# Layer A's three Strassen products: weight sums made of additions only, half of them by accumulating DMAs for 14 of 24 weight pairs

## The chip, the cores and the metric

One core of a Trainium2 chip runs the whole program. The metric is the device time in microseconds, as the median over runs. Engines are named as the profile names them: PE multiplies matrices, DVE is the vector engine, ACT the scalar engine, POOL is GpSimd (here it mostly issues DMAs), SP issues most of the loads.

## The reference

A trunk of two layers over 512 positions of width 2048, in float32. Only layer A matters here:

```python
proj = x @ w_in
q, k, v, gate, iq, ik, iw = jnp.split(proj, SPLITS_A, axis=-1)
...
o = from_blocks(lax.map(block_fn, (to_blocks(q), to_blocks(iq), to_blocks(iw), starts)))
return (o * jax.nn.silu(gate)) @ w_o
```

Three blocks of 512 output columns of `x @ w_in` are the subject: the second and third block of the gate, and the fourth block of the queries.

## The kernel before, in words

Every matrix product is made of float32 numbers split in two parts: `split` (line 142) makes the high part on ACT (a copy) and the low part on DVE (a subtraction), and `mm3` (line 146) issues three matmuls for each product of two split numbers. All instructions issued inside these helpers carry line 118 in the profile; the matmuls carry lines 147 to 149.

The order of PE's work is the program's. ACT and DVE keep program order for what is issued while `pinned` is set, and that holds for all that is told here. The DMAs of POOL are placed by the scheduler; POOL itself issues in order.

The three products of layer A (lines 1136 to 1155) are made by a Strassen-Winograd scheme. A 2048 x 512 block of weights is cut in two halves of rows and two halves of columns, and a product of 2x2 blocks is made with seven block products in seven PSUM banks instead of eight. The sums of the activations, four for each of eight rows of 128, were made earlier and lie split in SBUF. The sums of the weights are made as the weights arrive.

`strassen_items` (line 444) makes them. A unit is one pair of weight rows, 128 rows k and 128 rows k + 8 by 512 columns: one 512 KB load into a `raw` buffer, of which there are three. There are 8 units in a product, 24 in all; the texts number them 0 to 23. With q0, q1 the two column halves of row k and q2, q3 those of row k + 8, `prepare` (line 449) makes two sums on DVE, and the loop makes two more from these:

```python
dve.tensor_tensor(st[:, :, 0], two[0], two[2], ALU.add)
dve.tensor_tensor(st[:, :, 2], two[1], two[0], ALU.subtract)
...
dve.tensor_tensor(s2, s1, two[1], ALU.subtract)
dve.tensor_tensor(s4, two[3], s2, ALU.subtract)
```

The sums of a unit lie in a place of 128 x 1024 numbers, one of three that other work has left free: the two halves of F[0] (`two`, line 1096) and `t3`. Then, for each half of 128 columns, q1 to q3 and the four sums are split. After the second half's splits, `prepare` of the next unit follows (except at units 1, 9 and 17). `Ahead(..., 2)` keeps two halves, one unit, ahead of PE. `gemm_s` (line 557) takes one half after the other and issues seven `mm3` for each: 42 matmuls of 256 columns for a unit, 336 for a product. Its third pair of factors is the first that needs a sum.

Side work is taken from the deque `bg` at chosen steps of a product (`PUMPS`, line 1131; a step is one `mm3`, a product has 112). At the end of a product `combine` (line 583) copies three of the seven banks by ACT and adds the rest on DVE, which frees the banks for the next product; its five last additions, four SiLU and, for the two gate blocks, a 1 MB store by POOL (`held_g`, line 1155) go to `bg`. During the second product keys are transposed on PE (line 1118). At the start of the third, POOL loads half of a query block into F[0]'s first half (line 1148), and after it the other half (line 1157); the first reader of F[0] is `first_query` (line 1313), some steps into the next stage. `turned_rows` (line 978) ends with four small DMAs by POOL.

Of the kernel before, what the change touches and what calls it, by code (L numbers as in the profile page):

```python
# [51 lines left out]
def steps(gen, n):  # L52
    for _ in range(n):
        next(gen, None)
# [23 lines left out]
def trunk_kernel(  # L78
# [115 lines left out]
    def next_raw():  # L194
        while sent[0] < len(units) and len(raws) < (6 if homes and sent[0] in kv_units else 2 if sent[0] == 3 else 4 if 5 < sent[0] < 24 else 3):
            lent = kv_units.get(sent[0], 0)
            if sent[0] in first_units:
                raw = x_places[first_units[sent[0]] % 2]
            elif homes and lent % 2:
                raw = homes[lent // 2 % 3]  # L200
            else:
                raw = top.tile([128, 2, 512], F32, name="raw", tag="raw", bufs=3)
            unit = units[sent[0]]
            if len(unit) == 1:
                _, k, n = unit[0].shape
            else:
                k, n = 2, unit[-1]
            raw = raw.rearrange("p a n -> p (a n)")[:, : k * n].rearrange("p (k n) -> p k n", k=k)
            if len(unit) == 1:
                nc.sync.dma_start(raw, unit[0])  # L210
            else:
                src, a, b, c0, n = unit
                rows = src.rearrange("(k p) n -> p k n", p=128)
                step = b - a
                if sent[0] < 2:

                    for i, cut in enumerate(((0, H if sent[0] else NSEL, T), (0, T))):
                        for lo, hi in zip(cut, cut[1:]):
                            halves.append((raw[:, i, lo:hi], rows[:, a + i * step, c0 + lo : c0 + hi]))
                    if len(halves) == 6:  # L220
                        for n in (3, 5):
                            tc.keep_in_program_order(nc.scalar.dma_start(*halves[n]))
                        for n in (1, 4, 2, 0):
                            nc.sync.dma_start(*halves[n])
                elif isinstance(c0, tuple):

                    for half, out in enumerate(raw.rearrange("p k (h n) -> h p k n", h=2)):
                        at = D // 2 * half + c0[0]
                        nc.sync.dma_start(out, rows[:, a : b + 1 : step, at : at + n // 2])
                else:  # L230
                    loaded = nc.sync.dma_start(raw, rows[:, a : b + 1 : step, c0 : c0 + n])
                    if 2 < sent[0] < 6:
                        tc.keep_in_program_order(loaded)
            raws.append(raw)
            sent[0] += 1
        return raws.popleft()
# [244 lines left out]
    def strassen_stream(widths, wp, places=None):  # L481
        return Ahead(strassen_items(widths, wp, places), 2)

    def kv_items(room, first, later, third=None):

        made = [0, 0]
        temps = list(first)

        def temp():
            made[0] += 1  # L490
            return temps[made[0] % len(temps)]

        def parts(src):
            made[1] += 1
            if room[0] and made[1] in (3, 5):
                pair = room[0].pop()
            elif (room[0] is not None and made[1] < 5) or made[1] % 2 == 0:
                pair = weight_parts()
            else:
                pair = [  # L500
                    room[1].tile([128, 4, 128], F32R, name=n, tag=n, bufs=3).rearrange("p a n -> p (a n)")
                    for n in ("sh", "sl")
                ]
            split(*pair, src)
            return pair

        for k in range(8):
            raw = next_raw()
            for a in range(2):
                yield parts(raw[:, a])  # L510
        for _ in range(2 if third is None else 0):
            st = room[1].tile([128, 4 * H], F32, name="st", tag="st", bufs=2)
            temps.extend(st[:, n * T : (n + 1) * T] for n in range(2))
        temps.extend(third or ())
        for k in range(8):
            raw = next_raw()
            s3 = temp()
            dve.tensor_tensor(s3, raw[:, 0], raw[:, 1], ALU.subtract)
            yield parts(raw[:, 0])
            yield parts(s3)  # L520

        def sums():
            r0 = next_raw()
            r1 = next_raw()
            s1, s2, s4 = temp(), temp(), temp()
            dve.tensor_tensor(s1, r0[:, 1], r1[:, 1], ALU.add)
            dve.tensor_tensor(s2, s1, r0[:, 0], ALU.subtract)
            dve.tensor_tensor(s4, r1[:, 0], s2, ALU.subtract)
            return s2, s1, s4

        temps.extend(later)
        ready = sums()
        for k in range(8):
            three = ready
            for n, src in enumerate(three):
                if n == 2 and k < 7:
                    ready = sums()
                yield parts(src)
# [38 lines left out]
    def quarter(x, i, j0=0, rows=2):  # L577

        j = j0 + rows * (i % 2 == 0)
        t = H * (i in (1, 2))  # L580
        return x[:, j : j + rows, t : t + H]

    def combine(wp, M, dst, u=None):

        m1, m2, m6, m7, m5, m3, m4 = M
        if u is None:
            u = wp.tile([128, 2, H], F32, name="u", tag="u", bufs=1)
        u = u[:, : m1.shape[1]]
        c11, c22, c12, c21 = (dst(i) for i in range(4))
        pinned[0] = True  # L590
        act.activation(u, m1, AF.Copy)
        act.activation(c21, m7, AF.Copy)
        act.activation(c22, m5, AF.Copy)
        dve.tensor_tensor(c11, m2, u, ALU.add)
        dve.tensor_tensor(u, m6, u, ALU.add)
        pinned[0] = False

        def onto(c):
            dve.tensor_tensor(c, c, u, ALU.add)

        paced(dve.tensor_tensor, c12, m3, c22, ALU.add)
        return [
            lambda: dve.tensor_tensor(c22, c22, c21, ALU.add),
            lambda: dve.tensor_tensor(c21, c21, m4, ALU.subtract),
            *(lambda c=c: onto(c) for c in (c12, c21, c22)),
        ]
# [371 lines left out]
    def turned_rows(packed, back):  # L978

        sw = pq.tile([128, T], F32, name="sw", tag="sw", bufs=1)  # L980
        swapped.append(sw)

        def last():
            dve.tensor_tensor(packed, packed, sw, ALU.add)
            for h in range(4):
                nc.gpsimd.dma_start(back(h), packed[32 * h : 32 * h + 32])

        return [
            lambda: dve.stream_shuffle(sw, packed, HALF_SWAP_16),
            lambda: dve.tensor_tensor(sw, sw, Sq, ALU.mult),  # L990
            lambda: dve.tensor_tensor(packed, packed, Cq, ALU.mult),
            last,
        ]
# [101 lines left out]

    two = [flat[0][:, 4 * n : 4 * n + 4].rearrange("p a t -> p (a t)") for n in range(2)]
    pinned[0] = True
    items = strassen_stream([512] * 3, sp, [*two * 2, t3.rearrange("p a t -> p (a t)"), two[1]]).prime()
    pinned[0] = False
    steps(gemm, 2)  # L1100
    for j in range(2):
# [13 lines left out]
    def key_rows(g, rows=slice(0, 128)):  # L1115
        return Kf[rows, :, g * 128 : (g + 1) * 128]
# [19 lines left out]
    for n, g in enumerate((1, 2, 3)):  # L1136
        M = product_banks(1 - n)
        gemm = pumped_at(gemm_s(items, C3A, M), PUMPS[n])
        if n == 1:
            bg.extend(rounds[2:])  # L1140
            steps(gemm, 28)
            for k in range(4):
                turned = turn_keys(k)
                steps(gemm, 10)
                turned()
                steps(gemm, 6)
        if n == 2:
            nc.gpsimd.dma_start(F[0][:, 0:2], held_q[0][:, 0:2])
            bg.extend(turned_rows(KP, lambda g: key_rows(g, slice(0, 32))))
        run(gemm)  # L1150
        drain()
        if n < 2:
            bg.extend(combine(None, M, lambda i: quarter(F[3], i), u[:, :, 0:H]))
            bg.extend(lambda j=j: act.activation(F[3][:, j], F[3][:, j], AF.Silu) for j in range(4))
            bg.append(lambda g=g: nc.gpsimd.dma_start(held_g[g], F[3]))

    nc.gpsimd.dma_start(F[0][:, 2:4], held_q[0][:, 2:4])
    items = Ahead(rest_items(), 2).prime()
    spare_u = pq.tile([128, T], F32, name="wk", tag="wk", bufs=1).rearrange("p (j t) -> p j t", j=2)
    late = deque(combine(None, M, lambda i: quarter(F[3], i), spare_u))  # L1160
    pc_.close()
    pkv_ = ExitStack()
    pkv = pkv_.enter_context(ss(name="pkv", bufs=1, side="right"))
# [1105 lines left out]
```

## Time and profile before

| | us |
|---|---|
| three runs, median | 1814.47 |
| three runs, lowest and highest | 1814.08, 1816.0 |
| the profiled execution, its own time | 1815.21 |
| its span, first to last instruction | 1813.5 |
| PE busy | 1807.6 |
| DVE busy | 1543.4 |
| ACT busy | 1051.5 |
| POOL busy | 33.5 |

The profile is of one execution. Times in it count from the first instruction. Matmuls are pipelined: a matmul's duration is longer than the distance to the next, so the pace of PE is read from start to start. A DMA issued by POOL appears twice, as an instruction of POOL (the issue) and as a row with the time from issue to landing. In the columns of a timeline, "x2" means two like instructions in one row, and what stands in brackets is the idle time before it and what ended that.

### The profile page before, as it was taken

The numbers are of one execution on the slowest core, as the hardware profiler recorded it, in microseconds if no ns is written. First come the engines' busy times: TensorE is split into PE (matmuls) and PEld (weight loads), VectorE is DVE, ScalarE is ACT, GpSimd is POOL, SyncE is SP. The second block draws the span as 40 slices with busy tenths as digits, with TensorE's granted clock in tenths as the row PEclk, the third lists the DMA queues.
The fourth block names the chain that finished last, engine by engine and source line by source line (L and its number), as shares of the span: only waits on it lengthen the run. The fifth ranks groups of instructions, "written<-read, shape, count | busy, mean of one in ns | idle before, by whom it ended". The sixth has DMA issues, their size and how long they took to land.

```text
span 1813.5 us, 28260 instructions
## 1 busy us (share of the span) xinstructions
PE 1807.6 (100%) x10231; PEld 1594.5 (88%) x10231; DVE 1543.4 (85%) x3085; ACT 1051.5 (58%) x1953; POOL 33.5 (2%) x75
## 2 busy tenths in 40 slices
PE   9999999999999999999999999999999999999999
PEld 8888888999888899888888899998888889988898
DVE  7888999998888899975578998888877889997997
ACT  4555355466666544575356444468888854557644
POOL 0001110000000000000000000000000000000000
PEclk9999999999999999999999999999999999999999
DMA  6524575344331454333347533322122244434453
GB/s 216 157 79 140 164 230 176 105 129 147 127 94 47 108 126 143 115 103 105 124 128 243 181 104 105 106 87 88 60 69 81 70 117 124 144 117 141 124 148 122
DMA packets 123740, 226.40 MB, mean 125 GB/s; under 512 B 10512, under 2 KB 40208, under 8 KB 122064
## 3 DMA queue, kind: packets, MB, share of 16 engines
q1 hardware_dynamic: 119936, 209.25, 38.5%
q0 software_dynamic: 3376, 14.95, 2.5%
q8 instruction: 80, 1.31, 0.3%
q14 instruction: 60, 0.49, 0.1%
q10 hardware_dynamic: 288, 0.39, 0.1%
HBM read 205.42 MB, written 16.78 MB: 123 GB/s over the span
## 4 chain that ended last, share of the span: by engine, by line
PE 99%; DMA 1%; DVE 0%; ACT 0%; issue 0%; DVEq 0%; ACTq 0%
PE m L148 12%; PE m L147 12%; PE m L149 12%; PE g L147 10%; PE g L149 10%; PE g L148 10%; PE o L148 4%; PE o L149 4%; PE o L147 4%; PE q L149 2%; PE q L148 2%; PE q L147 2%; PE iq L149 1%; PE iq L148 1%; PE iq L147 1%; PE z L2062 1%
## 5 line engine op out<-in xcount | busy, mean ns | idle before, releaser
L118 ACT ACTIVATE wh<-raw 128x512 fp32r<-128x512 f32 (+3 forms) x561 | 309.3, 552 | 373.2 <-PE g L148 118.7
L118 DVE TENSOR_TENSOR wl<-raw,wh 128x512 fp32r<-128x512 f32 (+3 forms) x560 | 331.6, 593 | 108.7 <-ACT wh L118 101.5
L147 PE MATMUL g<-xh,wh 128*128 128x512 f32 (+1 forms) x816 | 317.2, 389 | 0.0
L148 PE MATMUL g<-xl,wh 128*128 128x512 f32 (+1 forms) x816 | 314.6, 385 | 0.0
L149 PE MATMUL g<-xh,wl 128*128 128x512 f32 (+1 forms) x816 | 314.5, 385 | 0.0
L149 PEld LDWEIGHTS g<-xh,wl 128*128 128x128 f32 x816 | 153.3, 188 | 31.1
L147 PEld LDWEIGHTS g<-xh,wh 128*128 128x128 f32 x816 | 153.4, 188 | 29.1 <-ACT wk L116 0.3
L148 PEld LDWEIGHTS g<-xl,wh 128*128 128x128 f32 x816 | 153.5, 188 | 28.7
L118 ACT ACTIVATE sh<-f 128x512 fp32r<-128x512 f32 x129 | 80.5, 624 | 109.4 <-DVE f L118 104.2
L147 PE MATMUL m<-xh,wh 128*128 128x256 f32 x400 | 113.3, 283 | 0.0
L149 PE MATMUL m<-xh,wl 128*128 128x256 f32 x400 | 113.2, 283 | 0.0
L148 PE MATMUL m<-xl,wh 128*128 128x256 f32 x400 | 113.2, 283 | 0.0
L147 PE MATMUL m<-c,sh 128*128 128x256 f32 x368 | 104.3, 283 | 0.0
L149 PE MATMUL m<-c,sl 128*128 128x256 f32 x368 | 104.3, 283 | 0.0
L148 PE MATMUL m<-c,sh 128*128 128x256 f32 x368 | 104.1, 283 | 0.0
L118 DVE TENSOR_TENSOR sl<-f,sh 128x512 fp32r<-128x512 f32 x129 | 88.9, 689 | 16.1 <-ACT sh L118 16.0
L149 PE MATMUL o<-xh,wl 128*128 128x512 f32 x256 | 99.7, 389 | 0.0
L147 PE MATMUL o<-xh,wh 128*128 128x512 f32 x256 | 99.6, 389 | 0.0
L148 PE MATMUL o<-xl,wh 128*128 128x512 f32 x256 | 99.6, 389 | 0.0
L147 PE MATMUL m<-xh,sh 128*128 128x256 f32 x336 | 95.2, 283 | 0.0
L149 PE MATMUL m<-xh,sl 128*128 128x256 f32 x336 | 95.1, 283 | 0.0
L148 PE MATMUL m<-xl,sh 128*128 128x256 f32 x336 | 95.1, 283 | 0.0
(456 smaller groups left out, 4786.6 us busy)
## 6 DMA issues: line engine op xcount, KB each, us to landing
raw<-w_in_a SPq DMA_DIRECT2D x95, 512.0 KB, 3.7
raw<-w_in_b SPq DMA_DIRECT2D x64, 512.0 KB, 3.8
raw<-w_ple_gate SPq DMA_DIRECT2D x44, 512.0 KB, 3.9
raw<-w_o_a SPq DMA_DIRECT2D x24, 512.0 KB, 4.7
raw<-w_o_b SPq DMA_DIRECT2D x24, 512.0 KB, 4.7
f<-w_in_a SPq DMA_DIRECT2D x16, 512.0 KB, 4.6
f<-w_kv_b SPq DMA_DIRECT2D x16, 512.0 KB, 4.8
raw<-w_kv_b SPq DMA_DIRECT2D x16, 512.0 KB, 4.5
```

Of the source, the lines that this page charges most:

```text
L118: ins = method(*args, **kw)
L147: pe.matmul(out, a[0], b[0], start=start, stop=False)
L148: pe.matmul(out, a[0], b[1], start=False, stop=False)
L149: pe.matmul(out, a[1], b[0], start=False, stop=stop)
L2062: pe.matmul(z, down if kb % 2 else tri, p, start=False, stop=n == 1, skip_group_check=True)
```

## The change

`added_items` takes the place of `strassen_items` in these three products. Its four sums are q0 + q1, q0 + q2, q0 + q2 + q1 and q0 + q2 + q1 + q3, without a subtraction; `combine_added` takes the changed signs into account, with the same number of instructions as `combine`. For units 7 to 20 the first two sums are not made on DVE. POOL issues three DMAs for such a unit, two units ahead: one writes q0 from DRAM to two neighbouring blocks of the place, then one adds q1 onto the first of them and one adds q2 onto the second. The 512 KB load of the unit into `raw` stays. The places are given out in another order: the two halves of F[0] in turn for units 0 to 6, then `t3` and the two halves in turn, and `t3` and the second half for the last three. F[0]'s first half is in use until unit 18, so its load moves from the start of the third product to after 84 of that product's 112 steps.

```diff
+    def added_items(src, columns, places, wp, sent_ahead):
+
+        n = len(columns) * 8
+
+        def send(u):
+            rows = src.rearrange("(k p) n -> k p n", p=128)
+            c0, st = columns[u // 8], places[u].rearrange("p (i n) -> p i n", i=4)
+            first, second = (rows[u % 8][:, c : c + H] for c in (c0, c0 + H))
+            nc.gpsimd.dma_start(st[:, 0:2], first.unsqueeze(1).broadcast_to([128, 2, H]))
+            nc.gpsimd.dma_start(st[:, 0], second, accum_op=ALU.add)
+            nc.gpsimd.dma_start(st[:, 1], rows[u % 8 + 8][:, c0 : c0 + H], accum_op=ALU.add)
+
+        def prepare(u):
+            q = next_raw().rearrange("p a (b n) -> p (a b) n", b=2)
+            st = places[u].rearrange("p (i n) -> p i n", i=4)
+            if u not in sent_ahead:
+                dve.tensor_tensor(st[:, 0], q[:, 0], q[:, 1], ALU.add)
+                dve.tensor_tensor(st[:, 1], q[:, 0], q[:, 2], ALU.add)
+            return q, st
+
+        ready = None
+        for u in range(n):
+            q, st = ready or prepare(u)
+            if u + 2 in sent_ahead:
+                send(u + 2)
+            dve.tensor_tensor(st[:, 2], st[:, 1], q[:, 1], ALU.add)
+            dve.tensor_tensor(st[:, 3], st[:, 2], q[:, 3], ALU.add)
+            for j in range(2):
...
+                split(qh, ql, q[:, 1:4, cut])
+                split(sh, sl, st[:, :, cut])
+                if j and u + 1 < n:
+                    ready = prepare(u + 1) if u % 8 else None
+                yield [(qh[:, i], ql[:, i]) for i in range(3)] + [(sh[:, i], sl[:, i]) for i in (1, 2, 0, 3)]
+
...
+    def combine_added(M, dst, u):
...
+        act.activation(u, m1, AF.Copy)
+        act.activation(c21, m7, AF.Copy)
+        act.activation(c22, m5, AF.Copy)
+        dve.tensor_tensor(c11, m2, u, ALU.add)
+        dve.tensor_tensor(u, m6, u, ALU.subtract)
+        pinned[0] = False
+        paced(dve.tensor_tensor, c12, m3, c22, ALU.subtract)
+        return [
...
     pinned[0] = True
-    items = strassen_stream([512] * 3, sp, [*two * 2, t3.rearrange("p a t -> p (a t)"), two[1]]).prime()
+    third = t3.rearrange("p a t -> p (a t)")
+    places = [two[n % 2] for n in range(7)] + [(third, two[1], two[0])[n % 3] for n in range(14)] + [third, two[1], third]
+    added = added_items(w_in_a, (C_G + 512, C_G + 1024, C_Q + 1536), places, sp, range(7, 21))
+    items = Ahead(added, 2).prime()
     pinned[0] = False
...
         if n == 2:
+            bg.extend(turned_rows(KP, lambda g: key_rows(g, slice(0, 32))))
+        if n == 2:
+            steps(gemm, 84)
             nc.gpsimd.dma_start(F[0][:, 0:2], held_q[0][:, 0:2])
-            bg.extend(turned_rows(KP, lambda g: key_rows(g, slice(0, 32))))
...
-            bg.extend(combine(None, M, lambda i: quarter(F[3], i), u[:, :, 0:H]))
+            bg.extend(combine_added(M, lambda i: quarter(F[3], i), u[:, :, 0:H]))
...
-    late = deque(combine(None, M, lambda i: quarter(F[3], i), spare_u))
+    late = deque(combine_added(M, lambda i: quarter(F[3], i), spare_u))
```

## Rows read from the trace of the kernel before

**Rows 1.** The page: span, busy times, granted clock in 40 slices.
```profile
span 1813.5 us, 28260 instructions
...
PE 1807.6 (100%) x10231; PEld 1594.5 (88%) x10231; DVE 1543.4 (85%) x3085; ACT 1051.5 (58%) x1953; POOL 33.5 (2%) x75
...
PEclk9999999999999999999999999999999999999999
```
**Rows 2.** Waits of PE: line, releaser, us in total, times, longest.
```profile
PE m L147 <- DVE u L118: 0.2, 1, 0.2
```
**Rows 3.** Stretches of the products: length, busy PE, PEld, DVE, ACT, POOL, clock, DMA share.
```profile
308.40:348.70 40.30, 40.30 (x337) 40.29 (x336) 37.38 (x72) 18.95 (x37) 0.00 (x0) 1.00 0.36 105
348.70:390.80 42.10, 42.10 (x355) 42.10 (x354) 37.88 (x81) 25.35 (x49) 1.08 (x2) 1.00 0.44 136
390.80:431.50 40.70, 40.53 (x338) 40.32 (x337) 35.41 (x73) 19.87 (x39) 3.28 (x6) 1.00 0.50 151
```
**Rows 4.** PE in order of time: start us, us, instruction.
```profile
308.41 0.28 PE L147 MATMUL m<-xh,wh 128*128 128x256 f32 x1
...
348.72 0.28 PE L147 MATMUL m<-xh,wh 128*128 128x256 f32 x1
...
391.73 0.28 PE L149 MATMUL m<-ca,sl 128*128 128x256 f32 x1
392.18 0.39 PE L147 MATMUL m<-ca,sh 128*128 128x256 f32 x1 [0.17 <-DVE u L118]
...
411.36 0.28 PE L147 MATMUL m<-xh,wh 128*128 128x256 f32 x1
```
**Rows 5.** DVE and ACT in order of time: units 5, 8 and 16.
```profile
332.65 0.69 DVE L118 TENSOR_TENSOR sl<-f,sh 128x512 fp32r<-128x512 f32 x1
...
343.50 0.76 DVE L118 TENSOR_TENSOR f<-raw 128x256 f32<-128x256 f32 x2
344.17 0.42 DVE L118 TENSOR_TENSOR f<-f,raw 128x256 f32<-128x256 f32 x1
...
345.80 0.69 DVE L118 TENSOR_TENSOR sl<-f,sh 128x512 fp32r<-128x512 f32 x1 [0.29 <-ACT sh L118]
...
387.32 0.42 DVE L118 TENSOR_TENSOR f<-f,raw 128x256 f32<-128x256 f32 x1
...
345.14 0.63 ACT L118 ACTIVATE sh<-f 128x512 fp32r<-128x512 f32 x1 [0.80 <-DVE f L118]
```
**Rows 6.** DMA landings: 385 to 397, 420 to 430, 528 to 542 us.
```profile
raw<-w_in_a SPq DMA_DIRECT2D x3, 512.0 KB, 3.7
f<-heldq POOLq DMA_DIRECT2D x1, 512.0 KB, 6.9
...
f<-heldq POOLq DMA_DIRECT2D x1, 512.0 KB, 5.1
f<-rp POOLq DMA_DIRECT2D x4, 64.0 KB, 2.1
...
raw<-w_in_a SPq DMA_DIRECT2D x1, 512.0 KB, 5.0
Sq<-heldg POOLq DMA_DIRECT2D x1, 256.0 KB, 3.3
...
rp<-heldg POOLq DMA_DIRECT2D x1, 256.0 KB, 4.2
```
**Rows 7.** POOL in order of time, and SP's waits between 300 and 430 us.
```profile
372.62 0.54 POOL L1155 DMA_DIRECT2D heldg<-f  x1 [122.03 <-DMA raw<-w_in_a]
387.03 0.54 POOL L1148 DMA_DIRECT2D f<-heldq  x1 [13.87 <-DVE sl L118]
421.57 0.54 POOL L1157 DMA_DIRECT2D f<-heldq  x1 [5.97 <-DVE sl L118]
...
SPq L231 <- DVE wl L118: 115.8, 24, 7.9
```

More of the change, by code (lines that the diff above doesn't have):

```diff
@@ L482, in strassen_stream @@
         return Ahead(strassen_items(widths, wp, places), 2)
+    def added_items(src, columns, places, wp, sent_ahead):
[22 more added lines that the diff above has]
+            for j in range(2):
+                wh = top.tile([128, 512], F32R, name="wh", tag="wh", bufs=3)
+                wl = top.tile([128, 512], F32R, name="wl", tag="wl", bufs=3)
+                sh = wp.tile([128, 4, 128], F32R, name="sh", tag="sh", bufs=3)
+                sl = wp.tile([128, 4, 128], F32R, name="sl", tag="sl", bufs=3)
+                qh, ql = (w.rearrange("p (b c) -> p b c", b=4)[:, 0:3] for w in (wh, wl))
+                cut = slice(j * 128, (j + 1) * 128)
+                split(qh, ql, q[:, 1:4, cut])
[3 more added lines that the diff above has]
+                yield [(qh[:, i], ql[:, i]) for i in range(3)] + [(sh[:, i], sl[:, i]) for i in (1, 2, 0, 3)]
     def kv_items(room, first, later, third=None):
@@ L581, in quarter @@
         return x[:, j : j + rows, t : t + H]
+    def combine_added(M, dst, u):
+        m1, m2, m6, m7, m5, m3, m4 = M
+        c11, c22, c12, c21 = (dst(i) for i in range(4))
+        pinned[0] = True
+        act.activation(u, m1, AF.Copy)
[6 more added lines that the diff above has]
+        return [
+            lambda: dve.tensor_tensor(c22, c22, c21, ALU.subtract),
+            lambda: dve.tensor_tensor(c21, c21, m4, ALU.add),
+            lambda: dve.tensor_tensor(c12, c12, u, ALU.subtract),
+            lambda: dve.tensor_tensor(c21, u, c21, ALU.subtract),
+            lambda: dve.tensor_tensor(c22, c22, u, ALU.add),
+        ]
     def combine(wp, M, dst, u=None):
```

## The prediction

> **What bounds the kernel now.** I read the page first, then what PE waited for, then the three products of the changed stage with PE, VectorE (DVE) and GpSimd (POOL) in order of time, and last the landing times of the DMAs that POOL issues. The page shows PE busy for 1807.6 of 1813.5 us at full granted clock in every slice [rows 1]. A busy PE need not be an efficient one, so the list of waits matters more: after the first microseconds the only stall of PE in it is one of 0.2 us, for a DVE result named u [rows 2]. The whole kernel is one chain of matmuls.
>
> The changed stage is the three Strassen products from 308.4 to 431.5 us. In each of them PE is busy throughout, while DVE is busy 37.4 of 40.3, 37.9 of 42.1 and 35.4 of 40.7 us and POOL nearly idle [rows 3]. So DVE is close behind PE but does not hold it: the first product starts at 308.41, the second at 348.72, which is 336 matmuls at 0.120 us, and from 392.18 to 411.36, the start of unit 20, the 159 matmuls (four units of 42, less the nine before) stand 0.121 us apart [rows 4]. A unit (42 matmuls; 24 units, numbered 0 to 23) takes PE 5.04 us. The one gap stands at 392.18, at the start of the third product, 0.45 instead of 0.12 us after its predecessor, released by DVE's u [rows 4].
>
> **The change, part by part.**
>
> Adds taken from DVE. Each unit has four adds of 128x256. The first two are the row "f<-raw x2" of 0.76 us, with the next instruction 0.67 us after its start (343.50 to 344.17) [rows 5]. Fourteen units lose that pair: 14 x 0.67 = 9.4 us of DVE time. On the path it gives back at most the one gap: 0.45 - 0.12 = 0.33 us, since PE otherwise runs at its own pace. I take -0.3 us. The two remaining adds, the splits and the combining instructions keep number and shape; only signs and order change, so they cost nothing new. PE's 1008 matmuls in the stage stay as they are.
>
> DMAs put in their place. For each of units 7 to 20 POOL issues three: a plain one that writes one 128x256 block twice (256 KB), then two accumulating ones of 128 KB into its two halves. Both accumulations must wait for the landing of the first, and POOL issues in order, so POOL stands still for that time and the next unit's chain waits behind it. That is the price to work out: P, POOL's time for one chain, and C, the time from a chain's start to its last landing.
>
> - First DMA, L1. Four plain 256 KB loads by POOL took 3.3 to 4.2 us from issue to landing (the first and the last of them stand there), in a stretch with few other loads; 512 KB loads took 5.1 and 6.9 us at the end and start of the third product, beside the weight loads [rows 6]. Bounds 3.3 and 6.9; I take 4.2, the largest at this size, because a 512 KB weight load of 3.7 us [rows 6] is under way in most of every 5.04 us here.
> - Accumulating DMA, L3. None in the trace. 64 KB took 2.1 us, 256 KB up to 4.2 us [rows 6]. It reads both source and destination, so I treat 128 KB as moving 256 KB, and take 3.7. Bounds 2.1 and 5.1 (the lower 512 KB row), the upper if adding slows the engines.
> - Issue. POOL's issues in this stage took 0.53 to 0.54 us each whatever the size [rows 7]; I take 0.55. An accumulating issue is not shown: from 0.53 to perhaps twice that.
> - Handover. ACT's split ends at 345.14 + 0.63 = 345.77 and DVE's starts at 345.80 [rows 5]; I round up to 0.1.
>
> So P = 4.2 + 2 x 0.55 + 0.1 = 5.4 us and C = 4.2 + 0.55 + 3.7 = 8.45 us. P is more than PE's 5.04 us: the chain alone cannot keep pace, and lives on its head start.
>
> The head start. Unit 8's place is free once unit 5's last split ends, 332.65 + 0.69 = 333.34 [rows 5]; unit 7's was free earlier. Unit 20's chain starts no sooner than 12 P later. It is needed when DVE begins unit 20's third add. In the trace that add of unit 8 starts at 344.17 and the first half's last split ends at 345.80 + 0.69 = 346.49, 2.32 us later [rows 5]; PE reads that result with the ninth matmul, 8 x 0.12 = 0.96 us after a unit's start. Unit 20 starts on PE at 411.36 [rows 4], so the latest start is 411.36 + 0.96 - 2.32 = 410.0. There are 410.0 - 333.3 = 76.7 us for 12 P + C = 64.8 + 8.45 = 73.3. It fits with 3.4 us to spare, and no stall results. At the product boundary the third product's banks are freed by instructions queued on DVE behind unit 16's splits, so unit 16 should be no later than now: its third add starts at 387.32 [rows 5], its chain lands at 333.3 + 8 x 5.4 + 8.45 = 385.0. Fits by 2.3 us.
>
> The new wait on DVE. If a chain is late, DVE stands at the third add; behind it in order are that unit's splits, the pumped side work and, at a boundary, the combining. ACT's second split, PE and SP's next weight load wait for those.
>
> POOL's other work. A 1 MB store at 372.62 and the query loads at 387.03 and 421.57 [rows 7] share the queue. A store queued one chain early holds the chains for up to its own wait; one P of 5.4 us would exceed the spare by 2.0 us, still within the "same" band. The first half of the query load moves from the start of the third product to after 84 of 112 steps, about 390.8 + 84 x 0.36 = 421 us; landing 6.9 us later gives 428, and its first reader is after the stage's end at 431.5. Cost 0; the cover is gone only if POOL is over 3 us behind there.
>
> Extra traffic. 14 x 512 KB written by POOL's queue beside weight loads that hold a DMA share of 0.36 to 0.50 [rows 3]; SP's loads wait for a weight buffer that DVE has not finished with, 115.8 us in the stage [rows 7], so they are early, and with three buffers at 5.04 us a unit a load that grows from 3.7 to 6 us stays hidden. Cost 0.
>
> Vector work against descriptors. The issues kept to 0.54 us although DVE was busy nine tenths of the stage [rows 3, 7], so I add nothing for interference. The Trainium skill, "SBUF — State Buffer", in the "DVE blocks DMA" trap, says that a VectorE operation using both ports keeps GpSimd from writing descriptors; by it each DMA could start one vector operation later. That speaks against this change, and it is rival 2 below.
>
> **Sum.** The profiled execution took 1815.21 us, 0.74 above the median of the three runs (1814.47). -0.3 +0 gives 1814.9 for it, 1814.2 as a median.
>
> **Rivals.**
> 1. POOL becomes the bound. The sum turns at 12 P + C = 76.7, with C = P + 3.05 at P = 5.67, that is L1 of 4.5 us, only 0.3 above what I take. With the 512 KB row's 5.1 us for L1 and 4.2 for L3: P = 6.3, C = 9.85, 75.6 + 9.85 - 76.7 = 8.8 us late, and each later unit is late with it: 1823.0. For it: the stage's own 512 KB rows and an issue price nobody has shown. Against: the 256 KB rows stay at 4.2 or below, one of the last beside a weight load [rows 6]. It is slower by over 3.6 us from 12 P + C = 80.3, P near 5.94. Chance 0.26.
> 2. Every POOL DMA pays one DVE instruction, 0.69 us, before its descriptors are written: P = 5.4 + 2.07 = 7.47, C = 10.5, 89.6 + 10.5 - 76.7 = 23.4 us: 1837.6. Issues of 0.54 us speak against it. Chance 0.04.
> 3. DVE was pacing PE without a row that says so; then 9.4 us come back: 1805. The even 0.12 us from matmul to matmul speaks against it [rows 4]. Chance 0.03.
>
> **How the numbers follow.** Forecast (no stall, gain of a few tenths): 0.67. A difference of 0.2%, 3.6 us, is about what a measurement of this kernel can tell from no change. Faster 0.03 (rival 3), same 0.67, slower 0.30 (rivals 1 and 2). The range starts at 1813.4, 0.8 below the forecast for the scatter of runs, and reaches 1823.0 to take in rival 1 at its worked price; rival 2, rival 3 and the 6.9 us end of L1 stay outside. Alone, the forecast's range is 1813.4 to 1816.5.
>
> **What would show it.** Right: DVE's busy time in the second and third product about 4 to 5 us lower each; matmuls 0.12 us apart to 431 us; POOL with chains of three issues every 5 to 5.4 us, the accumulating ones 4.2 us behind the first. Wrong: PE or DVE rows released by a DMA into f or t from unit 12 on; a first landing over 4.5 us or accumulating issues over 0.8 us; chains 6 us apart.

## The result, and the profile after

The changed kernel takes 1831.43 us (median of four runs, 1828.49 to 1832.69) beside 1814.49 us before (also four runs): a ratio of 1.009, 95% interval 1.0072 to 1.0107. It is slower by some 17 us. The forecast was no change, with a range that ended at 1823.0; the sign is that of rival 1, and the size is twice its price.

The page of the changed kernel: the span, and the busy times that answer to [rows 1].

```profile
span 1829.6 us, 28336 instructions
...
PE 1813.4 (99%) x10231; PEld 1598.4 (87%) x10231; DVE 1535.4 (84%) x3057; ACT 1050.3 (57%) x1953; POOL 68.6 (4%) x117
```

DVE lost 28 instructions and 8.0 us, as the edit says. PE made the same 10231 matmuls in a span that is 16.1 us longer. Its waits between 300 and 450 us (line, releaser, us in total, times, longest), where before there was one of 0.2 us [rows 2]:

```profile
PE m L149 <- DVE wl L118: 7.0, 5, 2.3
PE kt L1184 <- ACT rp L118: 1.9, 2, 1.6
PE m L147 <- ACT u L118: 1.3, 1, 1.3
PE m L147 <- DVE f L118: 0.4, 1, 0.4
```

PE now waits 10.6 us: for split weights, whose splits stand behind a unit's sums on DVE, for the copies of transposed keys and for the combining. Read from start to start, these nine waits cost some 12.0 us: the matmul before a wait is recorded with 0.28 us where the pace is 0.12 [rows 4], which hides 0.16 of each. By product, cut at the products' own first matmuls (columns as in [rows 3]: length, busy PE, PEld, DVE, ACT, POOL, granted clock, DMA share):

```profile
307.70:348.00 40.30, 40.30 (x338) 40.30 (x336) 36.34 (x68) 18.90 (x37) 8.29 (x10) 1.00 0.57 149
348.00:397.10 49.10, 44.62 (x354) 42.52 (x353) 29.92 (x57) 22.82 (x43) 18.00 (x22) 1.00 0.69 171
397.10:447.60 50.50, 44.35 (x339) 43.47 (x338) 36.37 (x71) 21.96 (x43) 13.15 (x18) 0.93 0.65 180
```

The first product is as long as before. The second is 7.0 us longer than its stretch of 42.1, the third 9.8 us longer than its 40.7; together 16.8 us, of which 0.7 are made up by an earlier start in this execution. In the third the granted clock is 0.93: about 0.07 x 50.5 = 3.5 us of its growth come from the clock and not from a wait.

DVE stands still before the third add of a unit, because the two sums that it reads have not landed. Here at units 13 and 18 (start us, us, idle before and releaser):

```profile
376.56 0.89 DVE L118 TENSOR_TENSOR t<-t,raw 128x256 f32<-128x256 f32 x2 [4.58 <-DMA t<-w_in_a]
...
414.64 0.88 DVE L118 TENSOR_TENSOR f<-f,raw 128x256 f32<-128x256 f32 x2 [4.01 <-DMA f<-w_in_a]
```

POOL's queue shows why they land late. Its instructions in order of time (start us, us, idle before and releaser); L492 is the first DMA of a chain, L493 and L494 the accumulating ones, L1220 the 1 MB store:

```profile
333.03 0.75 POOL L492 DMA_DIRECT2D f<-w_in_a  x1 [2.63 <-DVE sl L118]
337.26 0.87 POOL L493 DMA_DIRECT2D f<-w_in_a  x1 [3.48 <-DMA f<-w_in_a]
337.84 1.18 POOL L494 DMA_DIRECT2D f<-w_in_a  x1
338.38 1.39 POOL L492 DMA_DIRECT2D f<-w_in_a  x1
343.56 0.86 POOL L493 DMA_DIRECT2D f<-w_in_a  x1 [3.80 <-DMA f<-w_in_a]
...
378.85 1.37 POOL L492 DMA_DIRECT2D f<-w_in_a  x1
379.58 1.21 POOL L1220 DMA_DIRECT2D heldg<-f  x1
385.96 0.86 POOL L493 DMA_DIRECT2D f<-w_in_a  x1 [5.17 <-DMA f<-w_in_a]
...
400.97 1.37 POOL L492 DMA_DIRECT2D f<-w_in_a  x1
401.98 1.11 POOL L492 DMA_DIRECT2D t<-w_in_a  x1
...
410.33 1.91 POOL L492 DMA_DIRECT2D f<-w_in_a  x1
```

From unit 9's chain (338.38) to unit 18's (400.97) a chain's first DMA is issued right behind the two accumulating ones of the chain before, with no idle time, and these nine chains take 6.95 us each. Unit 19's first DMA (401.98) goes out 1.0 us behind unit 18's, ahead of its accumulating ones. From 338.38 to 410.33, eleven chains, POOL always has one under way, and one takes 6.5 us in the mean. PE's pace is 5.04. The landings of these DMAs and of the weight loads (raw) between 300 and 450 us (KB each, median us from issue to landing):

```profile
raw<-w_in_a SPq DMA_DIRECT2D x24, 512.0 KB, 4.4
f<-w_in_a POOLq DMA_DIRECT2D x9, 256.0 KB, 5.7
f<-w_in_a POOLq DMA_DIRECT2D x18, 128.0 KB, 3.9
...
t<-w_in_a POOLq DMA_DIRECT2D x5, 256.0 KB, 5.4
```

The 128 KB rows mix two kinds. By issuing line over all 14 chains, the first accumulating DMA (L493) and then the second (L494):

```profile
DMA to landing us min/median/max: 3.1/3.2/6.9
DMA to landing us min/median/max: 3.8/4.9/7.1
```

The second is issued 0.58 us behind the first and takes 1.7 us longer. It is the one that a unit's sums are complete with, and the plain DMA issued behind it lands 0.6 to 1.9 us after it.

The chain of waits of the same stretch runs through the first DMAs, one after the other (start us, us):

```profile
333.03 3.94 DMA f<-w_in_a
338.38 4.90 DMA f<-w_in_a
344.68 4.28 DMA t<-w_in_a
350.36 4.99 DMA f<-w_in_a
```

The two that find POOL idle, of units 7 (324.93) and 8 (333.03), land in 3.4 and 3.94 us; those behind accumulating DMAs take 4.3 to 7.0.

### The profile page after: what moved, and what is told of

It is laid out like the page before. It is cut to its first block, busy times and chain, and to the rows that moved or that the text cites. A ratio compares the mean times of both kernels' runs of the same rounds, so it can differ in the third digit from the quotient of the medians.

```text
span 1829.6 us, 28336 instructions
## 1 busy us (share of the span) xinstructions
PE 1813.4 (99%) x10231; PEld 1598.4 (87%) x10231; DVE 1535.4 (84%) x3057; ACT 1050.3 (57%) x1953; POOL 68.6 (4%) x117
## 4 chain that ended last, share of the span: by engine, by line
PE 93%; DMA 4%; DVE 1%; POOL 1%; issue 0%; ACT 0%; ACTq 0%; DVEq 0%
PE m L149 10%; PE m L148 10%; PE m L147 10%; PE g L147 10%; PE g L149 10%; PE g L148 10%; PE o L149 4%; PE o L148 4%; PE o L147 4%; DMA f<-w_in_a 3%; PE q L148 2%; PE q L149 2%; PE q L147 2%; PE iq L147 1%; PE iq L149 1%; PE iq L148 1%
## 5 line engine op out<-in xcount | busy, mean ns | idle before, releaser
L118 ACT ACTIVATE sh<-f 128x512 fp32r<-128x512 f32 x123 | 76.7, 624 | 122.2 <-DVE f L118 117.1
L118 DVE TENSOR_TENSOR sl<-f,sh 128x512 fp32r<-128x512 f32 x123 | 84.7, 689 | 16.6 <-ACT sh L118 16.4
```

Source lines behind the costliest of these rows:

```text
L118: ins = method(*args, **kw)
```

## The experiments

Two theories stood against each other: that the order of POOL's queue (it stands through every first landing) sets the pace, and that the DMAs themselves cost too much, through traffic or through the adding. Each kernel below is the changed one with one edit, timed in three rounds beside the kernel before on the same chip.

**All sums on DVE.** This leaves the new signs, the new places and the moved load of the query block in.

```diff
-    added = added_items(w_in_a, (C_G + 512, C_G + 1024, C_Q + 1536), places, sp, range(7, 21))
+    added = added_items(w_in_a, (C_G + 512, C_G + 1024, C_Q + 1536), places, sp, range(0))
```

> Theory (POOL's queue sets the pace: each chain holds POOL from the first DMA's issue to its landing plus two issues, and units fall behind PE's 5.04 us): with all sums on DVE and no DMAs for them, 1814.3 us, the time before, with matmuls 0.12 us apart. Rival (the new signs, the new order of the places or the moved query load cost the time): it stays near 1831 us.

1814.43 us, ratio 1.0001 (0.9991 to 1.001). Everything but the DMAs is free; the whole loss comes with the chains.

**Every second unit.**

```diff
-..., places, sp, range(7, 21))
+..., places, sp, range(8, 21, 2))
```

> Only units 8, 10, ... 20 are sent ahead, 7 chains for 14. Theory: a chain every 10 us leaves POOL free before the next, no lateness builds up, 1814.3 to 1815.5 us. Rival (each chain costs PE a fixed amount, 16 us / 14 = 1.15 us, through traffic or the adding): 7 x 1.15 = 8 us, 1822 us.

1813.8 us, ratio 0.9998 (0.9989 to 1.0008). A fixed cost for each chain is out. The first DMAs, now alone in POOL's queue, land sooner than in the changed kernel (5.7). Of the adding ones the first lands in 4.2 and the second in 4.3 (median; there 3.2 and 4.9):

```profile
f<-w_in_a POOLq DMA_DIRECT2D x5, 256.0 KB, 4.0
f<-w_in_a POOLq DMA_DIRECT2D x10, 128.0 KB, 4.2
```

**Only units 7 to 13.**

```diff
-..., places, sp, range(7, 21))
+..., places, sp, range(7, 14))
```

> Only units 7 to 13 are sent ahead. Theory: lateness is small for the first chains and grows with each; in the changed kernel PE's gaps up to unit 13 are 1.6 and 0.6 us, so 1816.5 us. Rival (a fixed cost for each chain): half of 16 us, 1822 us.

1819.61 us, ratio 1.0031 (1.0019 to 1.0042): 5.4 us, between the two expectations, and a miss for the theory's number. The trace says why. Unit 13's chain made DVE stand still for 3.88 us; PE then lost little. But units 14 and on have all their sums on DVE again, which is near PE's pace (DVE was busy nine tenths of these stretches before [rows 3]), so DVE did not make the delay good before the boundary, and PE paid at the start of the third product, where the combining frees its banks. DVE at unit 13, and PE around the boundary (columns as above):

```profile
374.17 0.89 DVE L118 TENSOR_TENSOR t<-t,raw 128x256 f32<-128x256 f32 x2 [3.88 <-DMA t<-w_in_a]
```

```profile
390.00:395.00 5.00, 3.46 (x26) 3.05 (x26) 4.54 (x10) 3.40 (x7) 0.00 (x0) 0.99 0.47 120
395.00:400.00 5.00, 5.00 (x30) 4.77 (x30) 4.64 (x10) 1.66 (x4) 0.00 (x0) 0.67 0.26 95
```

PE idles 1.54 us in the first of these, and in the next 5 us the granted clock is 0.67, which makes 30 matmuls out of 44: another 1.6 us. Two waits of 0.6 us in all came before. Read from start to start, all four waits and the clock make 4.4 of the 5.4 us; the last 1 us is not settled.

**Traffic without a reader.** DVE makes all sums, in the two halves of F[0]; the chains run into `t3`, which nobody reads.

```diff
-            c0, st = columns[u // 8], places[u].rearrange("p (i n) -> p i n", i=4)
+            c0, st = columns[u // 8], aside.rearrange("p (i n) -> p i n", i=4)
...
-            if u not in sent_ahead:
-                dve.tensor_tensor(st[:, 0], q[:, 0], q[:, 1], ALU.add)
-                dve.tensor_tensor(st[:, 1], q[:, 0], q[:, 2], ALU.add)
+            dve.tensor_tensor(st[:, 0], q[:, 0], q[:, 1], ALU.add)
+            dve.tensor_tensor(st[:, 1], q[:, 0], q[:, 2], ALU.add)
...
+    places = [two[n % 2] for n in range(24)]
```

The cut leaves out that the query load, which the change had moved to 84 steps, is issued only behind the third product, since F[0]'s first half is now in use to the end.

> All sums are made by DVE; the 14 chains run as in the change but into a place that nobody reads. Theory: POOL's chains still take 5 to 7 us each, but nothing waits for them, 1814.3 to 1815.5 us. Rival (the added traffic delays weight loads or the places): over 1820 us.

1847.44 us, ratio 1.0176 (1.0161 to 1.0191), which looks like the rival and is not. With one place each chain also waits for its predecessor's last landing, so a chain takes about 10 us, and the two 1 MB stores of gate blocks stand behind them in POOL's queue, the first until 397.00 instead of 372.62 [rows 7]. DVE's combining waits for the stores and PE for DVE. DVE's wait, and PE's two:

```profile
DVE f L118 <- DMA heldg<-f: 30.1, 2, 17.1
```

```profile
PE g L147 <- DVE f L118: 15.2, 1, 15.2
PE m L147 <- DVE f L118: 13.1, 1, 13.1
```

So it was repeated with two places in turn, and with the stores on ACT's queue; the rest is as in the run above:

```diff
+            c0, st = columns[u // 8], aside.rearrange("p (i n) -> p i n", i=4)[:, u % 2 * 2 : u % 2 * 2 + 2]
...
-            bg.append(lambda g=g: nc.gpsimd.dma_start(held_g[g], F[3]))
+            bg.append(lambda g=g: tc.keep_in_program_order(nc.scalar.dma_start(held_g[g], F[3])))
```

> The 14 chains again run for nobody, now into two places in turn, all sums on DVE, and ACT's queue instead of POOL's issues the 1 MB stores, so that nothing of the stage stands behind a chain. Theory (only what waits for a chain, or stands behind one in POOL's queue, loses time): 1814.3 to 1815.5 us, with chains that take POOL 5 us or more each. Rival (the traffic of the chains slows weight loads or PE): over 1820 us.

1814.26 us, ratio 1.0003 (0.9994 to 1.0012). All 42 DMAs run beside the three products, the last of them is issued at 397.57, and PE loses nothing. The traffic is free when nobody waits for it. It is the same traffic and not the same order: POOL issues some first DMAs ahead of the adding ones of the chain before, and begins a chain every 5.2 us. Whether the second place or the moved stores made the difference to 1847 us was not tried apart.

**SP issues the first DMA.**

```diff
-            nc.gpsimd.dma_start(st[:, 0:2], first.unsqueeze(1).broadcast_to([128, 2, H]))
+            nc.sync.dma_start(st[:, 0:2], first.unsqueeze(1).broadcast_to([128, 2, H]))
```

> SP issues the first DMA of each chain, POOL only the two accumulating ones. Theory: POOL no longer stands between a chain's first issue and the next chain, and the first DMA does not queue behind the accumulating ones of the chain before; 1814.5 to 1817 us. Rival (the accumulating DMAs themselves are too slow): stalls of over 5 us stay, 1820 us or more.

1813.57 us, ratio 0.9997 (0.9988 to 1.0007). The landings are about as long in sum as in the changed kernel (5.7 and 3.9):

```profile
f<-w_in_a SPq DMA_DIRECT2D x9, 256.0 KB, 4.5
f<-w_in_a POOLq DMA_DIRECT2D x18, 128.0 KB, 5.0
```

A chain still takes 4.5 + 0.6 + 5.0, about 10 us from first issue to last landing. It no longer matters, since POOL is not held while the first DMA is under way.

**POOL's order.** The first DMA of unit u + 2 goes ahead of the adding ones of unit u + 1.

```diff
             if u + 2 in sent_ahead:
-                send(u + 2)
+                send(u + 2, False)
+            if u + 1 in sent_ahead:
+                send(u + 1, True)
```

The cut leaves out that `send` is divided in two and that its DMAs are pinned in program order.

> POOL issues the first DMA of unit u + 2 ahead of the accumulating ones of unit u + 1, so that it does not stand through a whole landing. Theory: 1814.5 to 1818 us. Rival (the DMA engines or the adding are the limit, not the order of the queue): 1826 us or more.

1814.55 us, ratio 1.0001 (0.9992 to 1.0011), with the same 42 DMAs on the same queue. The order alone cures it. But for the adding ones of two chains, POOL now waits for a place to come free, not for a landing:

```profile
352.55 0.75 POOL L493 DMA_DIRECT2D f<-w_in_a  x1 [2.80 <-DVE sl L118]
353.28 0.90 POOL L495 DMA_DIRECT2D f<-w_in_a  x1
353.86 1.20 POOL L496 DMA_DIRECT2D f<-w_in_a  x1
```

**One adding DMA for two.** The same bytes, one issue less.

```diff
-            nc.gpsimd.dma_start(st[:, 0], second, accum_op=ALU.add)
-            nc.gpsimd.dma_start(st[:, 1], rows[u % 8 + 8][:, c0 : c0 + H], accum_op=ALU.add)
+            both = second.unsqueeze(1).broadcast_to([128, 2, H])
+            both = bass.AP(both.tensor, both.offset, [both.ap[0], [8 * 128 * src.shape[1] - H, 2], both.ap[2]])
+            nc.gpsimd.dma_start(st[:, 0:2], both, accum_op=ALU.add)
```

> The two accumulating DMAs of a chain become one with the same bytes. Theory: one issue of 0.55 us less on POOL for each chain, 12 x 0.55 = 6.6 us less lateness, 1823 to 1826 us. Rival (bytes set the landing times, the issue does not matter): 1830 us.

1832.81 us, ratio 1.0101 (1.0082 to 1.0121): no gain, a miss for the theory. What is saved at the issue is not gained in full: from unit 9's chain to unit 18's (337.82 to 398.12) one takes 6.70 us, 0.25 less than the 6.95 of the changed kernel. And that is lost again at unit 19, whose first DMA waits its turn here (404.71, 6.6 us behind unit 18's, there 1.0). One of the chains, with 7.0 us from start to start, of which POOL stands idle for 5.03:

```profile
350.26 1.19 POOL L492 DMA_DIRECT2D f<-w_in_a  x1
356.48 1.19 POOL L495 DMA_DIRECT2D f<-w_in_a  x1 [5.03 <-DMA f<-w_in_a]
357.22 1.17 POOL L492 DMA_DIRECT2D f<-w_in_a  x1
```

**Plain writes for adding ones.** The same queue, order and bytes written; the additions of 14 units are left out.

```diff
-            nc.gpsimd.dma_start(st[:, 0], second, accum_op=ALU.add)
-            nc.gpsimd.dma_start(st[:, 1], rows[u % 8 + 8][:, c0 : c0 + H], accum_op=ALU.add)
+            nc.gpsimd.dma_start(st[:, 0], second)
+            nc.gpsimd.dma_start(st[:, 1], rows[u % 8 + 8][:, c0 : c0 + H])
```

> The second and third DMA of each chain write instead of adding, so the additions q0 + q1 and q0 + q2 are left out for 14 units. Theory: the order of the queue and its waits are the same; 1827 to 1832 us. Rival (the adding inside the DMA is what is slow, and holds up the next chain's first DMA): the first landing falls to 4.2 us and the time to 1814 to 1818 us.

1814.1 us, ratio 0.9998 (0.9989 to 1.0008): the rival's number. Here too a first DMA is issued right behind the two of the chain before, and it lands in 3.9 us instead of 5.7. The two behind the first take 3.6 us each, instead of 3.2 and 4.9 (last rows: L493, L494):

```profile
raw<-w_in_a SPq DMA_DIRECT2D x26, 512.0 KB, 3.7
f<-w_in_a POOLq DMA_DIRECT2D x9, 256.0 KB, 3.9
f<-w_in_a POOLq DMA_DIRECT2D x18, 128.0 KB, 3.7
...
DMA to landing us min/median/max: 3.1/3.6/5.8
DMA to landing us min/median/max: 2.9/3.6/5.5
```

```profile
338.67 0.71 POOL L492 DMA_DIRECT2D f<-w_in_a  x1
...
395.53 0.71 POOL L492 DMA_DIRECT2D f<-w_in_a  x1
```

From unit 9's chain to unit 20's, eleven chains in 56.9 us are 5.2 us each. That is still above PE's 5.04, but little enough for the head start to last.

The adding shows in the DMA engines too. POOL's queue between 300 and 450 us, in the changed kernel and here (packets, MB, the time of the packets as a share of 16 engines): the same bytes in fewer packets and two thirds of the time.

```profile
q0 software_dynamic: 5856, 10.75, 31.6%
```

```profile
q0 software_dynamic: 3168, 10.75, 21.0%
```

How the adding lengthens the landings is open in part. From unit 12's chain to unit 17's, the changed kernel's next weight load is issued 0.2 to 1.4 us behind the chain's first DMA (at 371.35 behind 371.11) and takes 4.9 to 9.3 us; the two are under way together. Here it is mostly issued ahead of the two plain DMAs (at 368.17 before 368.32) and takes 3.7 us as a median. How much of the 1.8 us between 3.9 and 5.7 is the adding and how much the weight load beside it was not tried apart. The first three landings behind adding DMAs, before PE's first wait, took 4.3 to 5.0 us.

So both theories hold in part: the queue's order makes a chain's time count, and with adding DMAs that time is 6.5 us, with plain ones 5.2. Either cure is enough.

**The store out of POOL's queue.**

```diff
-            bg.append(lambda g=g: nc.gpsimd.dma_start(held_g[g], F[3]))
+            bg.append(lambda g=g: tc.keep_in_program_order(nc.scalar.dma_start(held_g[g], F[3])))
```

> The changed kernel with the two 1 MB stores issued by ACT's queue, which takes the first of them out from between the chains of units 15 and 16 in POOL's. Theory (the pace of the chains): one issue of 0.5 us and at most the 1.9 us by which the chain beside the store is longer than the mean of 6.5: 1829 to 1831 us. Rival (the store is what holds the chains up): 1820 us or less.

1829.53 us, ratio 1.0076 (1.006 to 1.0093). It is 1.9 us less than the changed kernel, and the intervals overlap: the store is a detail of some 2 us at most.

No version beats the kernel before beyond what a measurement can tell. The best, with SP, is 0.6 us under it, inside its interval; PE does not wait in its three products.

## Why the prediction was wrong

- **What bounds the kernel** was right. Without the DMAs the time is that of before, and where the chains come in time (by SP, or in the other order) the 8.0 us taken from DVE (forecast 9.4) give PE nothing that can be measured.
- **The mechanism and its turning point** were right: POOL stands through each first landing, and units fall behind. The text let the sum turn at a pace of 5.67 us for a chain. The plain writes, at 5.2 us, lose nothing; the adding ones, at 6.5, lose 17 us.
- **The term that failed is L1, the landing of the first DMA.** The step took 4.2 us, "the largest at this size", from DMAs behind no adding one. Measured: 5.7 us as a median in the changed kernel, 4.3 to 7.0 behind adding DMAs; 4.0 to 4.4 alone (every second unit), 3.9 and 3.8 behind two plain ones. It is the landing for which POOL stands still, so each chain pays it. L3 was too small as well where it counts: 3.7 taken, 3.2 measured for the first adding DMA, but 4.9 for the second, which completes a unit's sums. The bound for slow adding (5.1) was set on L3 alone; the DMA behind had none. Issues and handover, 1.2 taken, are 1.4: 0.28 from landing to issue, then 0.58 and 0.54.
- **With the measured terms the prediction's sum gives the delay.** Unit 8's chain starts at 333.03 and unit 20's at 410.33: 77.3 us for 12 P, 64.8 forecast. Unit 20's third add starts at 424.77, when its chain has landed: C = 14.4, 8.45 forecast, since its first DMA took 7.0 and its last 6.5 us. That is 91.7 against the 76.7 that were to be had, 15.0 us late; PE comes to unit 20 at 427.42, 16.1 us later than before. The check at unit 16 failed likewise: its third add was to find the chain landed at 385.0 and starts at 398.29.
- **What the sum had no term for** is what a late PE costs on top: the granted clock of 0.93 in the third product, some 3.5 us. With the 12.0 us of waits that leaves 16.1 - 12.0 - 3.5 = 0.6 us, which is not settled; some of it lies in matmuls that are recorded longer just after a gap.
- **Rival 1's price** of 8.8 us rested on an L1 of 5.1 and left the clock out. Its chance of 0.26 was too small: the room was 0.3 us of L1, and no row showed a DMA behind an adding one.
- **Rival 2** is not seen: in the run with plain writes POOL's 128 KB issues took 0.54 to 0.57 us with DVE at work. **Rival 3** is out: DVE's 8.0 us brought nothing back.
- The store and the moved load were rightly held for small; the traffic too.

## What to carry to other kernels

A DMA queue that must wait for its own landings has a pace, and it is to be compared with the consumer's: here 6.5 us in the mean for a chain against 5.04 us for a unit, where the latency alone (10 us, two units ahead) would have been hidden. Where a chain has a dependent step, issue the next chain's independent step ahead of it, or give the two to different queues. A landing time read from a DMA that had the queue to itself is too low for one that follows an accumulating DMA (here 3.4 to 3.9 us against 4.3 to 7.0).

## What had not been expected of the hardware

An accumulating DMA of 128 KB is not slow by itself: the first of two took 3.2 us in the changed kernel and 4.2 in the run with every second unit (plain: 3.6). What follows it was: the second took 4.9 us (plain: 3.6), and a plain 256 KB DMA behind both 5.7 (behind two plain ones: 3.9), though a weight load under way at the same time may have its share. Making one DMA of the two does not cure it: the run with one adding DMA takes 1832.81 us. The Trainium skill, "Collectives: The Full Stack", in "The bandwidth ceiling: the fold count and why AG ≠ RS ≠ AR", is about reductions between cores; it puts the slowness of ReduceScatter down to the two reads that an addition needs, both queued on the same ring, and not to the adding. The runs here agree in so far as the same bytes take more packets (5856 for 3168) and the DMAs queued behind pay; they do not show the reads.

The granted clock fell behind short gaps. In the changed kernel PE stood 2.2 us and then 1.3 us shortly before 401.4; in the next 5 us the granted clock is 0.72, and matmuls start 0.21 us apart instead of 0.12. Granted clock between 400 and 405 us, and between 415 and 420, after a gap of 2.3 us (columns as above):

```profile
400.00:405.00 5.00, 3.36 (x15) 3.00 (x15) 3.57 (x6) 2.69 (x6) 3.09 (x4) 0.72 0.63 114
...
415.00:420.00 5.00, 3.95 (x21) 3.95 (x22) 4.69 (x10) 1.98 (x4) 2.22 (x3) 0.66 0.35 77
```

A gap of 1.6 us at 372.9 was not followed by a fall (1.00 from 370 to 380), while in the run with units 7 to 13 gaps of 1.2 and 0.4 us were (0.67). The length of a gap alone does not tell; the runs do not show what does.
